# A streaming encoder on one core: super-blocks that begin with a row job, a planner with a slack, and a new order of jobs

## The chip, the cores and the metric

The kernel runs on one core of one Trainium2 chip. The metric is the device time of one execution in microseconds (us). Three runs of the kernel before gave 1244.92, 1247.65 and 1249.84 us; the median is 1247.65 us. Engines are named as in the profile: PE is TensorE's matmuls, PEld its weight loads, DVE VectorE, ACT ScalarE, POOL GpSimd, SP SyncE, which issues the DMAs.

## What is computed

One layer of an encoder with two parallel groups of heads: chunked attention (group A) and a gated recurrence (group B), for 2048 frames of a new stream (the prompt) and 64 frames of a running one (the sample).

```python
def mixer_layer(x, ln_g, w_in, lb, norm_g, w_out, attn_fn, s0):
    aq, ak, av, ag, hq, hf, hi, hg = jnp.split(rms_norm(x, ln_g) @ w_in, SPLITS, axis=-1)
    o_a = attn_fn(heads(aq), heads(ak), heads(av)).reshape(B, T, W_A) * jax.nn.silu(ag)
    o_b, S = hgrn2_branch(hq, hf, hi, hg, lb, norm_g, s0)
    return x + jnp.concatenate([o_a, o_b], axis=-1) @ w_out, k, v, S
```

`x` is 2112 rows of 1024 features, `w_in` is 1024 x 4096, `w_out` 1024 x 1024. Attention has 8 heads of 64; each chunk of 64 frames sees itself and 8 chunks before it, with a bias by distance; for the sample, 512 rows of keys and values come from a cache. The recurrence has 4 heads of 128 and works in blocks of 32 frames. A final RMS norm gives the outputs; new keys, values and states are outputs too. All is float32, to a precision that one pass of the float32r matmul does not reach: every operand is split into a high and a low part, and three products (high x high, low x high, high x low) are added.

## The kernel before

**Super-blocks.** The frames are worked in four super-blocks of 512 (`SUPER`, here 0 to 3); number 1 holds the 64 sample frames as well (576 columns, worked as 256 + 320, while the others are worked as 512). The normalised rows of a super-block are transposed into `xh` and `xl` (high and low part, 8 tiles of 128 features) by `x_tile` and `x_split`; a super-block is filled half by half.

**Jobs.** A job is one projection of 128 output features: 24 matmuls (3 products by 8 tiles of features) with the weight tile stationary, `project`. `hf`, `hq`, `hi`, `hg` are the recurrence's forget gate, query, input and output gate for head 0 to 3; `pq`, `pk`, `pv`, `pg` are queries, keys, values and gate of attention's head pair 0 to 3. A weight tile `w` holds high and low part, 1 MB; there are four (`WBUFS`). In super-block 0 the weights are read raw, split on VectorE and GpSimd, and kept in DRAM (`wd`, `wvd`); later super-blocks load them back. In super-blocks 1 to 3 the `pv` and `hi` jobs of two pairs and two heads are done together as a *row job* `rv0` or `rv1`, `project_rows`: there `x` is stationary and four weight tiles stream through, 512 columns at a time, so that the result has frames in its partitions. It needs all four weight tiles at once, goes over the frames in four tiles of 128 (two per half; in super-block 1 a sample pass lies between the halves) in *quarters* of 6 matmuls, and gives each weight tile back near its end. Its output goes through `row_out`: ScalarE copies it to a `sig` buffer and splits it to a `vT` buffer (two of each), and SyncE writes both to scratch in DRAM (`irow`, `vrow`), from where the recurrence (`gi`) and attention (`v`) load them. A buffer is free again when its DMA has landed.

**Which job uses which buffer.** Results wait in two PSUM banks `acc`. Jobs of kind h and `pg` are read out by ScalarE into `sig`; `pq` and `pk` into `vT`. The sample's key cache is loaded into `ck` and transposed on TensorE (`sample_cache`), for each head pair in super-block 1.

**What sets the order.** `JOBS` gives the order of the jobs by hand. The rest (recurrence, attention, transposes, output products) are Python generators that a planner, `Plan`, runs beside the jobs while the program is built: `main` walks through the jobs and `pump` lets every generator go on whose wanted time has come. The planner keeps a clock (`now`, TensorE's) and charges each instruction with an estimated cost; what it decides is fixed in the program as the order of the instructions of each engine. On the chip only semaphores count. `Tok` counts free buffers, with the planned time at which each is given back.

**The start of a super-block.** The first two jobs (`u < 2`) are worked by halves, first both jobs on half 0, then both on half 1, so that they can begin before the second half of `x` is there: `first`, line 2393. The last job of super-blocks 0 to 2 is worked by halves too.

Of the kernel before, what the change touches and what calls it, by code (L numbers as in the profile page):

```python
# [44 lines left out]

ROWSB = (1, 2, 3)
JOBS = [[(x[:2], int(x[2])) for x in jobs.split()] for jobs in (
# [8 lines left out]
)]  # L56


class Plan:
# [4 lines left out]

    LAG = {"": 0.0, "T": 200.0, "A": 100.0, "D": 100.0, "P": 100.0, "S": 100.0}
    TURN = 160.0

    def __init__(self):
        self.now = 0.0
        self.free = {"A": 0.0, "D": 0.0, "P": 0.0, "S": 0.0}  # L70
        self.done = {"A": 0.0, "D": 0.0, "P": 0.0, "S": 0.0}
        self.turns = {"D": [], "P": []}
        self.links = 0.0
        self.landed = 0.0
        self.mode = None
        self.run = 0
        self.breath = None
        self.threads = []
        self.count = 0
        self.rooms = {}  # L80
        self.seen = {}

    def spawn(self, gen, prio=1):
        self.count += 1
# [12 lines left out]
    def _when(self, want):  # L97


        if isinstance(want, tuple):  # L100
            return max(want[1], self.free[want[0]] - QUEUE)
        if isinstance(want, Tok):
            return want.when()
        return want

    def pump(self):
        moved = True
        any_ = False
        while moved:
            moved = False  # L110
            for th in list(self.threads):
                while self._ready(th[3]):
                    moved = any_ = True
                    try:
                        th[3] = next(th[2])
                        if th[3] is None:
                            th[3] = self.now + 1.0
                    except StopIteration:
                        self.threads.remove(th)
                        break  # L120
                if moved:
                    break
        return any_
# [6 lines left out]

    def main(self, gen):
        for want in gen:
            self.pump()
# [8 lines left out]
    def drain(self):  # L142
        while self.threads:
            if not self.pump():
                self.skip()
# [112 lines left out]
class Queue:  # L258
# [32 lines left out]
    def cost(self, name, aps, kw):  # L291
# [61 lines left out]
class Tok:  # L353


    def __init__(self, plan, n):
        self.plan = plan
        self.at = [0.0] * n

    @property  # L360
    def n(self):
        return sum(t <= self.plan.now for t in self.at)

    def when(self):
        return min(self.at) if self.at else NEVER

    def take(self):
        self.at.remove(min(self.at))
# [11 lines left out]
def hymba_step(  # L380
# [68 lines left out]
    def mm32(out, w, x):  # L449
        pe.matmul(out, w, x, start=True, stop=True)  # L450

    tk = {k: Tok(C, n) for k, n in dict(acc=2, s_ps=1, tr=2, pv=1, g=1, pr=PRB, ph=2, sig=2, vT=2, mixa=2,
                                     w=WBUFS, raw=RAWB, xn=XNB, qk=1, kv=1, q=1, sga=2, bias=1, gf=1, gi=1, gg=1,
                                     ck=1, slot=4, x4=0, x5=0, rec=1).items()}

# [351 lines left out]

    row_n = {}

    def project_rows(j, sb, r):  # L810


        ws = []
# [46 lines left out]
        for c0 in (0, 2 * P):  # L860
# [3 lines left out]
            steps = [(0, 0), (0, 1), (0, 2), (0, 3), (1, 0), (1, 1), (1, 2), (1, 3)]  # L864
            if c0:
                steps = [(0, 0), (0, 1), (0, 2), (1, 0), (1, 1), (0, 3), (1, 2), (1, 3)]
            for a, i in steps:
                c = c0 + a * P
                if a == len(accs):
                    yield from tk["acc"].get()  # L870
                    accs.append(acc_ps())
                yield from quarter(accs[a], c, i)
                if c0 and a:
                    tk["w"].put(1, C.pe())
                if i == 3:
                    C.spawn(row_out(sb, r, accs[a], c // P, C.pe()), 0)
# [1413 lines left out]
    def program():  # L2290
# [74 lines left out]
        for sb in range(nsb):  # L2365
# [6 lines left out]
            for u, (kind, g) in enumerate(JOBS[sb]):  # L2372
# [9 lines left out]
                            for c in range(off, off + bn, P):  # L2382
                                C.spawn(x_tile(sb + 1, half, c), 0.5)
                if kind == "rv":
                    yield from project_rows(j, sb, g)
                    j += 4
                    continue
                if (kind[0], g) not in made:
# [174 lines left out]
```

## Time and profile before

| | |
|---|---|
| runs | 1244.92, 1247.65, 1249.84 us |
| profiled execution | 1248.5 us, of which the span is 1246.7 us |
| mean granted clock of TensorE | 0.995 |
| DMA | 288.74 MB, 232 GB/s over the span |
| chain that ended last, by engine | PE 80%, DMA 5%, DVE 4%, the rest 1% each or less |

Nearly all instructions show one line (L273), since one helper records them; they are told apart by the tiles they write and read (out<-in). A row `MATMUL acc<-xh,w 128*128 128x512 f32` is a matmul into a bank of `acc` with 512 columns. Where matmuls follow each other the length of one (389 ns) is longer than the distance of their starts, since they are pipelined; what a matmul costs is read from the distance. Super-block 1 runs from about 260 us to about 545 us of the span.

### The profile page before, as it was taken

The numbers are of one execution on the slowest core, as the hardware profiler recorded it, in microseconds if no ns is written. First come the engines' busy times: TensorE is split into PE (matmuls) and PEld (weight loads), VectorE is DVE, ScalarE is ACT, GpSimd is POOL, SyncE is SP. The second block draws the span as 40 slices with busy tenths as digits, with TensorE's granted clock in tenths as the row PEclk, the third lists the DMA queues.
The fourth block names the chain that finished last, engine by engine and source line by source line (L and its number), as shares of the span: only waits on it lengthen the run. The fifth ranks groups of instructions, "written<-read, shape, count | busy, mean of one in ns | idle before, by whom it ended". The sixth has DMA issues, their size and how long they took to land.

```text
span 1246.7 us, 21739 instructions
## 1 busy us (share of the span) xinstructions
PE 1224.7 (98%) x7804; PEld 1062.6 (85%) x7804; DVE 894.6 (72%) x1864; ACT 694.6 (56%) x1520; POOL 374.3 (30%) x697
## 2 busy tenths in 40 slices
PE   9999999998999999999999999999999999999997
PEld 8788888988998899998888888998888888888786
DVE  7678887762876199798277857981878367887886
ACT  6344655552765187675357567772655446643443
POOL 7666647110122011111254541151112011741110
PEclk9999999998999999999999999999999999999999
DMA  8888996739354655542986797758454784997431
GB/s 294 276 277 310 313 323 215 256 105 329 126 190 161 227 177 200 193 137 93 382 306 220 273 368 279 259 200 310 186 175 165 250 322 162 362 308 203 127 135 68
DMA packets 126349, 288.74 MB, mean 232 GB/s; under 512 B 11745, under 2 KB 73057, under 8 KB 109602
## 3 DMA queue, kind: packets, MB, share of 16 engines
q1 hardware_dynamic: 126098, 287.09, 66.0%
q8 instruction: 62, 1.02, 0.3%
q14 instruction: 45, 0.37, 0.1%
q10 hardware_dynamic: 144, 0.26, 0.1%
HBM read 198.06 MB, written 90.83 MB: 232 GB/s over the span
## 4 chain that ended last, share of the span: by engine, by line
PE 80%; DMA 5%; DVE 4%; ACT 1%; POOL 1%; issue 1%; SPq 0%; DVEq 0%; ACTq 0%; POOLq 0%
PE acc L273 58%; PE g L273 7%; PE tr L273 6%; PE pv L273 5%; PE s L273 5%; POOL w L273 1%; DMA wraw<-in_w_in_dram 1%; DMA w<-wvd 1%; DMA ck<-in_cache_attn_k_dram 1%; DMA v<-vrow 1%; DVE xn L273 1%; DMA vrow<-vT 1%; DVE pr L273 1%; DMA w<-wd 1%; ACT sig L273 0%
## 5 line engine op out<-in xcount | busy, mean ns | idle before, releaser
L273 PE MATMUL acc<-xh,w 128*128 128x512 f32 (+2 forms) x2176 | 460.1, 351 | 3.1 <-ACT vT L273 2.3
L273 PEld LDWEIGHTS acc<-xh,w 128*128 128x128 f32 x2176 | 354.3, 190 | 46.4 <-ACT vT L273 2.5
L273 PE MATMUL acc<-xl,w 128*128 128x512 f32 (+2 forms) x1088 | 235.5, 350 | 0.0
L273 PEld LDWEIGHTS acc<-xl,w 128*128 128x128 f32 x1088 | 179.0, 191 | 21.7
L273 PE MATMUL acc<-w,xh 128*128 128x512 f32 x400 | 130.8, 396 | 1.7 <-DMA w<-wvd 1.7
L273 ACT ACTIVATE pr<-pr,nm 128x640 f32<-128x640 f32 (+4 forms) x132 | 100.4, 761 | 46.0 <-DVE nm L273 45.5
L273 ACT CAST ph<-tr 128x512 fp32r<-128x512 f32 (+3 forms) x176 | 87.2, 507 | 65.5 <-PE tr L273 33.0
L273 POOL TENSOR_TENSOR w<-wraw,w 128x256 fp32r<-128x256 f32 x120 | 104.4, 897 | 54.1 <-DVE w L273 31.9
L273 DVE CUSTOM_DVE_ANT_0 pr<-s,bias 128x640 f32<-128x640 f32 (+5 forms) x144 | 100.7, 703 | 21.2 <-PE s L273 20.4
L273 DVE TENSOR_TENSOR ph<-tr,ph 128x512 fp32r<-128x512 f32 (+3 forms) x176 | 101.3, 589 | 15.8 <-ACT ph L273 14.8
L273 PE MATMUL pv<-ph,v 128*128 128x256 f32 (+2 forms) x344 | 97.4, 373 | 0.5 <-DMA v<-vrow 0.2
L273 POOL TENSOR_TENSOR k<-ob 128x512 f32<-128x512 f32 (+2 forms) x20 | 18.2, 908 | 263.8 <-ACT ob L273 249.4
L273 ACT ACTIVATE sig<-acc 128x256 f32<-128x256 f32 (+2 forms) x87 | 42.9, 493 | 89.1 <-PE acc L273 86.0
L273 PE MATMUL tr<-ident,pr 128*128 128x128 f32 x580 | 89.0, 273 | 1.1 <-DVE ph L273 1.1
L273 PEld LDWEIGHTS acc<-w,xh 128*128 128x128 f32 x400 | 74.1, 188 | 16.4 <-DMA w<-wvd 2.6
L273 DVE TENSOR_SCALAR pr<-pr,sm 128x640 f32<-128x640 f32 (+4 forms) x132 | 79.6, 603 | 4.7
L273 PEld LDWEIGHTS tr<-ident,pr 128*128 128x128 f32 x580 | 70.0, 140 | 11.3 <-DVE ph L273 1.4
L273 PE MATMUL acc<-w,xl 128*128 128x512 f32 x200 | 78.3, 391 | 0.0
L273 POOL TENSOR_TENSOR mixa<-mixa,sga 128x256 f32<-128x256 f32 (+1 forms) x36 | 28.7, 796 | 131.2 <-DVE mixa L273 102.2
L273 DVE TENSOR_TENSOR mixa<-mixa,pv 64x256 f32<-64x256 f32 (+1 forms) x144 | 56.8, 395 | 14.1 <-ACT mixa L273 8.9
L273 PEld LDWEIGHTS pv<-ph,v 128*128 128x128 f32 x344 | 58.0, 189 | 9.7 <-issue 1.4
L273 ACT ACTIVATE sig<-sig 128x512 f32<-128x512 f32 (+2 forms) x110 | 57.7, 525 | 15.0 <-DVE gk L273 12.2
(326 smaller groups left out, 2209.0 us busy)
## 6 DMA issues: line engine op xcount, KB each, us to landing
w<-wd SPq DMA_DIRECT2D x72, 1024.0 KB, 6.6
wd<-w SPq DMA_DIRECT2D x24, 1024.0 KB, 6.9
w<-wvd SPq DMA_DIRECT2D x24, 1024.0 KB, 5.0
wraw<-in_w_in_dram SPq DMA_DIRECT2D x30, 512.0 KB, 5.4
wod<-xn SPq DMA_DIRECT2D x28, 512.0 KB, 5.6
v<-vrow SPq DMA_DIRECT2D x24, 512.0 KB, 7.8
xn<-in_x_prompt_dram SPq DMA_DIRECT2D x23, 512.0 KB, 5.5
wvd<-w SPq DMA_DIRECT2D x16, 512.0 KB, 7.0
```

Of the source, the lines that this page charges most:

```text
L273: r = f(*args, **kw)
```

## The change

Four edits. The order of the jobs is new, and super-blocks 1 to 3 begin with `rv0`. The first two jobs of a super-block that begins so are not worked by halves any more; the row job itself goes, in its first half, over both tiles of frames for each weight tile in turn. The planner holds a thread's wanted time and the return of PSUM banks back by 200 ns (`MARGIN`), unless nothing else can be issued. And GpSimd's instructions with two inputs are charged more in the planner's table of costs above 257 columns.

```diff
-    "hf0 hq0 rv0 hg0 pq0 pk0 hf1 pg0 hq1 hg1 pg1 hf2 pq1 hq2 rv1 pk1 hg2 pg2 pq2 pk2 hq3 hg3 pg3 hf3 "
-    "pk3 pq3",
+    "rv0 hf0 hg0 pg0 pq0 hq0 pk0 hf1 hq1 hg1 pg1 pk1 pq1 rv1 hf2 hq2 pg2 pq2 pk2 hg2 hf3 hq3 pq3 hg3 "
+    "pg3 pk3",
...
+    MARGIN = 200.0
+    BANKS = ("acc", "s_ps", "tr", "pv", "g")
...
-        return want
+        return want + self.margin
...
-                            th[3] = self.now + 1.0
+                            th[3] = ("", self.now + 1.0)
...
         for want in gen:
+            self.margin = self.MARGIN
             self.pump()
             while not self._ready(want):
                 if not self.pump() and not self._ready(want):
+                    if self.margin:
+                        self.margin = 0.0
+                        continue
...
-            return min(200.0 + 2.1 * n, 432.0 + 1.2 * n), 43.0 if n > 128 else 66.0, True
+            pairs = name in ("tensor_tensor", "tensor_mul", "tensor_sub")
+            return (200.0 + 2.1 * n if pairs else min(200.0 + 2.1 * n, 432.0 + 1.2 * n)), 43.0 if n > 128 else 66.0, True
...
-        return sum(t <= self.plan.now for t in self.at)
+        return sum(t + self.late() <= self.plan.now for t in self.at)
...
             if c0:
                 steps = [(0, 0), (0, 1), (0, 2), (1, 0), (1, 1), (0, 3), (1, 2), (1, 3)]
+            elif first:
+                steps = [(a, i) for i in range(4) for a in range(2)]
...
-                first, end = u < 2, not last and u >= len(JOBS[sb]) - 1
+                first, end = u < 2 and JOBS[sb][0][0] != "rv", not last and u >= len(JOBS[sb]) - 1
```

Where this moves instructions is seen in three places. The names are tiles with the building's numbers; L273 of the kernel before and L281 of the changed one are the same helper.

**First place: the loads and the cache's transposes behind `rv0` of super-block 1.** SyncE's DMAs, before, from the first load of head pair 0 on (`kd` keys, `v` values, `bias`, `ck` the key cache, `w` a weight tile, `gi` the recurrence's input):

```order
L273 DMA kd_3475<-carry_0_18_91 128x2x512
L273 DMA v_3478<-vrow_30_103 128x1024
L273 DMA bias_3481<-biasd_40_113 128x1280
L273 DMA ck_3485<-in_cache_attn_k_dram 128x4x128
L273 DMA w_3494<-wd_56_129 128x2048
L273 DMA gi_3431<-irow_35_108 128x512
L273 DMA gi_3431<-ilast_112 64x128
L273 DMA v_3478<-vrow_31_104 128x1024
```

and in the changed kernel:

```order
L281 DMA w_3299<-wd_60_133 128x2048
L281 DMA gi_3249<-irow_35_108 128x512
L281 DMA gi_3249<-ilast_112 64x128
L281 DMA kd_3365<-carry_0_18_91 128x2x512
L281 DMA v_3368<-vrow_30_103 128x1024
L281 DMA v_3368<-vrow_31_104 128x1024
L281 DMA v_3368<-vlast_111 64x256
L281 DMA bias_3373<-biasd_40_113 128x1280
L281 DMA ck_3377<-in_cache_attn_k_dram 128x4x128
```

A weight tile, the recurrence's input and the second part of `v` now stand ahead of `ck`. TensorE's rows up to the transposes of `ck`, before (the job `acc_3545` is the second half of the second job behind the row job):

```order
L273 MATMUL acc_3545<-xh_168,w_3382 128x320 x2
L273 MATMUL g_3552<-ident_71,bl_3249 128x128 x2
L273 MATMUL acc_3545<-xh_168,w_3382 128x320 x6
L273 MATMUL acc_3545<-xl_169,w_3382 128x320 x8
L273 MATMUL acc_3545<-xh_168,w_3382 128x320 x4
L273 MATMUL tr_3577<-ident_71,ck_3485 128x128 x4
```

and in the changed kernel, where `acc_3379` and `acc_3411` are the two blocks of the third job behind the row job and `acc_3442` begins the fourth (the two jobs ahead of them stand without anything between):

```order
L281 MATMUL acc_3379<-xh_168,w_3218 128x256 x8
L281 MATMUL acc_3379<-xl_169,w_3218 128x256 x8
L281 MATMUL acc_3379<-xh_168,w_3218 128x256 x8
L281 MATMUL acc_3411<-xh_168,w_3218 128x320 x8
L281 MATMUL acc_3411<-xl_169,w_3218 128x320 x8
L281 MATMUL acc_3411<-xh_168,w_3218 128x320 x8
L281 MATMUL acc_3442<-xh_168,w_3228 128x256 x8
L281 MATMUL acc_3442<-xl_169,w_3228 128x256 x8
L281 MATMUL acc_3442<-xh_168,w_3228 128x256 x8
L281 MATMUL acc_3474<-xh_168,w_3228 128x320 x4
L281 MATMUL tr_3481<-ident_71,ck_3377 128x128 x4
```

The transposes moved from the second job behind the row job to the fourth.

**Second place: ScalarE behind `rv1` of super-block 1.** Before, after the last two outputs of the row job (`sig` and `vT` from `acc`), the key job `pk1` follows:

```order
L273 COPY sig_5052<-acc_4999 128x512
L273 CAST vT_5054<-sig_5052 128x2x2x64
L273 COPY sig_5071<-acc_5027 128x512
L273 CAST vT_5073<-sig_5071 128x2x2x64
L273 COPY vT_5133<-acc_5076 128x256
L273 CAST kd_4414<-vT_5133 64x256 x2
```

and in the changed kernel the forget gate `hf2`:

```order
L281 COPY sig_5225<-acc_5101 128x512
L281 CAST vT_5227<-sig_5225 128x2x2x64
L281 COPY sig_5249<-acc_5156 128x512
L281 CAST vT_5251<-sig_5249 128x2x2x64
L281 ACTIVATE sig_5287<-acc_5246 128x256
L281 ACTIVATE sig_5287<-sig_5287,one_79 128x256
```

The first read-out behind the row job now takes a `sig` buffer where it took a `vT` buffer.

**Third place: TensorE at the start of super-block 2.** Before, `hf0` (`acc_6813`) and `hq0` (`acc_6878`) on half 0, 256 columns, with transposes (`tr`, `g`) and attention scores (`s`) between:

```order
L273 MATMUL acc_6813<-xh_168,w_6380 128x256 x6
L273 MATMUL tr_6824<-ident_71,xn_6701 128x128 x4
L273 MATMUL acc_6813<-xh_168,w_6380 128x256 x2
L273 MATMUL acc_6813<-xl_169,w_6380 128x256 x6
L273 MATMUL s_6848<-kd_6281,q_6282 128x320 x2
L273 MATMUL s_6848<-kd_6281,ql_170 128x320 x2
L273 MATMUL acc_6813<-xl_169,w_6380 128x256 x2
L273 MATMUL acc_6813<-xh_168,w_6380 128x256 x8
L273 MATMUL g_6872<-ident_71,xn_6701 128x128 x4
L273 MATMUL acc_6878<-xh_168,w_6499 128x256 x8
```

and in the changed kernel the first quarters of `rv0`, 512 columns, on two tiles of frames (`acc_6844`, `acc_6889`):

```order
L281 MATMUL acc_6844<-w_6382,xh_168 128x512
L281 MATMUL acc_6844<-w_6382,xl_169 128x512
L281 MATMUL g_6872<-ident_71,bl_6725 128x128 x2
L281 MATMUL g_6872<-ident_71,bl_6725 64x128
L281 MATMUL acc_6844<-w_6382,xh_168 128x512
L281 MATMUL acc_6844<-w_6382,xl_169 128x512
L281 MATMUL acc_6844<-w_6382,xh_168 128x512 x2
L281 MATMUL acc_6889<-w_6382,xh_168 128x512
L281 MATMUL acc_6889<-w_6382,xl_169 128x512
```

The eight pieces of `hf0` and `hq0` by halves are gone from the start; these jobs follow behind the row job with 512 columns. In the whole program TensorE has 192 matmuls of 256 columns less and 96 of 512 columns more; no other form changes its count.

More of the change, by code (lines that the diff above doesn't have):

```diff
@@ L66 @@
     TURN = 160.0
+    MARGIN = 200.0
+    BANKS = ("acc", "s_ps", "tr", "pv", "g")
     def __init__(self):
         self.now = 0.0
-        self.free = {"A": 0.0, "D": 0.0, "P": 0.0, "S": 0.0}
+        self.free = {"": 0.0, "A": 0.0, "D": 0.0, "P": 0.0, "S": 0.0}
         self.done = {"A": 0.0, "D": 0.0, "P": 0.0, "S": 0.0}
@@ L132, in main @@
         for want in gen:
+            self.margin = self.MARGIN
             self.pump()
@@ L142, in drain @@
     def drain(self):
+        self.margin = 0.0
         while self.threads:
@@ L353, with __init__, late @@
 class Tok:
-    def __init__(self, plan, n):
+    def __init__(self, plan, n, bank=False):
         self.plan = plan
+        self.bank = bank
         self.at = [0.0] * n
+    def late(self):
+        return self.plan.margin if self.bank else 0.0
     @property
     def n(self):
-        return sum(t <= self.plan.now for t in self.at)
+        return sum(t + self.late() <= self.plan.now for t in self.at)
     def when(self):
-        return min(self.at) if self.at else NEVER
+        return min(self.at) + self.late() if self.at else NEVER
     def take(self):
@@ L450, in mm32 @@
         pe.matmul(out, w, x, start=True, stop=True)
-    tk = {k: Tok(C, n) for k, n in dict(acc=2, s_ps=1, tr=2, pv=1, g=1, pr=PRB, ph=2, sig=2, vT=2, mixa=2,
+    tk = {k: Tok(C, n, k in C.BANKS) for k, n in dict(acc=2, s_ps=1, tr=2, pv=1, g=1, pr=PRB, ph=2, sig=2, vT=2, mixa=2,
                                      w=WBUFS, raw=RAWB, xn=XNB, qk=1, kv=1, q=1, sga=2, bias=1, gf=1, gi=1, gg=1,
@@ L808, in hymba_step, with project_rows @@
     row_n = {}
-    def project_rows(j, sb, r):
+    def project_rows(j, sb, r, first):
         ws = []
@@ L2384, in program @@
                 if kind == "rv":
-                    yield from project_rows(j, sb, g)
+                    yield from project_rows(j, sb, g, u == 0)
                     j += 4
```

12 rows, old and new, of the table JOBS are left out of this document.

## The prediction

> **What bounds the kernel now.** I read the page first.
>
> ```profile
> span 1246.7 us, 21739 instructions
> PE 1224.7 (98%) x7804; PEld 1062.6 (85%) x7804; DVE 894.6 (72%) x1864; ACT 694.6 (56%) x1520; POOL 374.3 (30%) x697
> ```
>
> TensorE (PE) is busy for 98% of the span; the next engine, VectorE, for 72%. So the time is TensorE's work plus the 22 us in which it stands still, and a part of that is the start and the end of the program. A change of order can win only standing time and cheaper forms of the same matmuls. Next I read who TensorE waits for (columns: waiting tile, releaser, us in total, times, longest).
>
> ```profile
> PE tr L273 <- DMA ck<-in_cache_attn_k_dram: 3.3, 1, 3.3
> PE acc L273 <- ACT vT L273: 2.3, 1, 2.3
> PE acc L273 <- DMA w<-wvd: 1.7, 2, 1.1
> PE s L273 <- DVE nm L273: 1.4, 4, 0.8
> PE tr L273 <- DVE ph L273: 1.1, 2, 0.8
> PE g L273 <- POOL breath L458: 1.1, 1, 1.1
> PE g L273 <- DVE asb L273: 1.0, 2, 0.6
> PE acc L273 <- DVE xn L273: 0.9, 2, 0.5
> PE acc L273 <- ACT sig L273: 0.8, 1, 0.8
> PE g L273 <- ACT k L273: 0.4, 1, 0.4
> ```
>
> These ten rows add up to 14.0 us, and three waits (3.3, 2.3, 1.1) are nearly half of it. All three lie in super-block 1. The timeline of TensorE gives their places (start, length, instructions, then the idle time ahead in brackets), the windows the clock that was granted around them (window, its length, PE busy, PEclk, DMA share, GB/s).
>
> ```profile
> 287.88 1.19 PE L273 MATMUL acc<-xh,w 128*128 128x256 f32 x8
> ...
> 301.23 0.75 PE L273 MATMUL acc<-xh,w 128*128 128x320 f32 x4
> 305.31 1.11 PE L273 MATMUL tr<-ident,ck 128*128 128x128 f32 x4 [3.33 <-DMA ck<-in_cache_attn_k_dram]
> ...
> 400.52 0.50 PE L273 MATMUL acc<-w,xh 128*128 128x512 f32 x1 [1.12 <-DMA w<-wvd]
> ...
> 421.97 1.12 PE L273 MATMUL acc<-xh,w 128*128 128x256 f32 x8
> ...
> 426.02 1.34 PE L273 MATMUL acc<-xl,w 128*128 128x320 f32 x8
> 427.19 1.33 PE L273 MATMUL acc<-xh,w 128*128 128x320 f32 x8
> 430.80 1.59 PE L273 MATMUL acc<-xh,w 128*128 128x256 f32 x6 [2.27 <-ACT vT L273]
> ```
>
> ```profile
> 302.00:306.00 4.00, 0.69 (x3) 0.83 1.03 405
> 306.00:310.00 4.00, 4.00 (x20) 0.50 0.81 249
> 310.00:314.00 4.00, 4.00 (x29) 0.82 0.50 202
> 398.00:402.00 4.00, 2.88 (x13) 1.00 0.56 229
> 429.00:433.00 4.00, 2.20 (x10) 0.74 1.04 412
> 433.00:437.00 4.00, 4.00 (x56) 0.84 0.52 174
> ```
>
> Each of the two long waits is followed by a stretch at half clock. Its length is (1 - PEclk) / 0.5 x 4 us, summed: 1.36 + 4.00 + 1.44 = 6.80 us after the first, 2.08 + 1.28 = 3.36 us after the second. The first began at 306 - 1.36 = 304.64 and TensorE stood idle until 305.31, so 6.13 us of work ran at half speed and lost 3.07 us; the second lost 1.68 us. The wait of 1.12 us has no such tail (398.00:402.00).
>
> The rows at 287.88 and 421.97 are the first job behind a row job each: the row jobs end there.
>
> What ended the three waits is in the chain of waits (start, us, what).
>
> ```profile
> 294.81 10.46 DMA ck<-in_cache_attn_k_dram
> 395.32 5.16 DMA w<-wvd
> 421.22 9.06 DMA vrow<-vT
> ```
>
> The cause is the same at 294.81 and 421.22: both lie just behind a row job. Its four weight tiles come free almost together, four loads of 1 MB fill the queue (DMA share 1.03), and the transfer that is needed next stands behind them.
>
> **The change part by part. Halves.** In super-blocks 2 and 3 the first two jobs now run in halves of 256 columns; behind a row job they run as one of 512. Four jobs of 48 matmuls become four of 24: 192 matmuls of 256 columns out, 96 of 512 in (super-block 1 is cut in two anyway).
>
> ```profile
> 422.93 1.12 PE L273 MATMUL acc<-xl,w 128*128 128x256 f32 x8
> 423.89 2.30 PE L273 MATMUL acc<-xh,w 128*128 128x256 f32 x16
> 1095.34 54.55 PE acc L273 x240
> ```
>
> Starts at 422.93 and 423.89 with 8 matmuls between give 120 ns for 256 columns; 54.55 / 240 gives 227.3 ns for 512 (the last row is of the chain). 192 x 120 - 96 x 227.3 = 23.04 - 21.82, so **-1.22 us**. TensorE is the bound there, so nothing hides it.
>
> The Trainium skill, "TensorE: Matmul & The Clock Gate", section "Wait — 56ns, not 53.3ns?", gives a warm matmul N / 2.4 GHz plus about 2.5 ns, which makes two halves only 2.5 ns dearer than one whole; by that rule this term would be 0.24 us and the sum 1.0 us higher. The trace has 120 and 227 ns, and I go by the trace.
>
> **The wait at 430.80.** The row job's outputs sit in the two `sig` and two `vT` buffers until their DMAs to scratch land. In the present order a key job (`pk1`) follows the second row job of super-block 1 and needs `vT` at once.
>
> ```profile
> 291.92 0.39 ACT L273 ACTIVATE sig<-acc 128x256 f32<-128x256 f32 x1 [2.96 <-DMA irow<-sig]
> ...
> 430.38 0.37 ACT L273 COPY vT<-acc 128x256 f32<-128x256 f32 x1 [7.18 <-DMA vrow<-vT]
> ```
>
> ScalarE waited 7.18 us for `vrow<-vT`, both banks of `acc` stayed full, TensorE stopped. In the new order every row job is followed by jobs of kind h; the ScalarE rows shown above (second place) have `sig` there. `sig` waits for `irow<-sig`, which cost ScalarE 2.96 us at 291.92 and TensorE nothing. So this wait goes, with its clock: 2.27 + 1.68 = **-3.95 us**. Late next is `irow`: the third rival.
>
> The same page of the Trainium skill, section "What's actually happening", lets the clock fall only after an idle window of about 3.4 us. By that rule 2.27 us would not have done it, and this term would be 2.27 alone, the sum 1.7 us higher. The rows at 429 and 433 show that it did, so I price waits over 2 us with their clock.
>
> **The wait at 305.31.** `ck` stays behind the weight loads, and the SyncE rows shown above put one weight load and one `v` load more ahead of it. But its transposes move back. Before, TensorE came to them at 301.98, 14.1 us after the row job's end (287.88). Now three whole jobs and more lie between: a job of super-block 1 is 24 x 120 ns + 24 x 146 ns (8 matmuls of 320 columns from 426.02 to 427.19) = 6.39 us, so 3 x 6.39 + 2.88 + 4 x 0.146 = 22.6 us. `ck` landed at 305.27, 17.4 us after the row job; 1.5 MB more at the 405 GB/s of the window make 21.1 us. It is there 1.5 us early, as an estimate. So 3.33 + 3.07 = **-6.40 us** goes. The second row job of super-block 1 now has the same train behind it, `ck` again on its end, at about the same distance. An estimate that is 1.5 us early can miss: bounds are 0 and 6.40 us for each of the two, and I take 0.5 each, **+1.0 us**, nearer to the row worked out.
>
> **The wait at 400.52.** The fourth weight tile of that row job took 5.16 us from its slot's release and was waited for 1.12, so only some 4 us of work lay between. In the new order more work lies between: **-1.12 us**. Row jobs at a start run their two halves' quarters in turn and need the fourth tile after six quarters in place of three.
>
> **The slack.** 200 ns between the planned end of an operand and its use on TensorE can remove short waits for VectorE and ScalarE: `nm`, `ph`, `asb`, `k` are 3.9 us in 9 waits. At most 9 x 0.2 = 1.8; below, a gain can be lost where the plan then finds other work out of turn. I take the middle, **-0.9 us**.
>
> **New waits.** Any new order has some of its own. The trace cannot show them; bounds are 0 and one long wait with its clock (6.40). I take one of the common size, **+1.12 us**.
>
> The corrected cost of GpSimd's two-operand instructions in the planner and job order 0 move work that is not on TensorE's path (POOL is busy 30%): nothing, within the last bound. Sum, against the profiled execution's 1248.5 us (span 1246.7 plus 1.8): 1248.5 - 1.22 - 3.95 - 6.40 - 1.12 - 0.9 + 1.0 + 1.12 = **1237.0 us**. The median of the three runs is 0.85 us lower than that execution; I leave the sum as it is, inside their spread of 4.9.
>
> **The rivals.** *The queue wins again.* `ck` or another load is still late behind four weight loads, at one or both row jobs of super-block 1. For it: DMA shares of 1.03 and 1.04, and two loads more ahead of it. Against: 22.6 us of work in place of 14.1. One such wait with its clock gives 1237.0 + 6.4 - 0.5 = 1242.9, two 1248.8.
>
> *The change does not do what it says.* The slack and the order only rename the waits, since transfers are late by microseconds and the slack is 0.2. Left is the halves' term: 1247.3.
>
> *Slower: `irow` blocks ScalarE.* ScalarE works in order, and the first activation of the second job after a row job waits until the last `irow<-sig` has landed.
>
> ```profile
> 298.38 0.32 SPq L273 DMA_DIRECT2D gi<-irow  x1
> 433.47 0.33 SPq L273 DMA_DIRECT2D gi<-irow  x1
> ...
> 293.33 0.42 DVE L273 TENSOR_TENSOR gg<-acc,sig 128x256 f32<-128x256 f32 x1 [3.91 <-ACT sig L273]
> ```
>
> The two loads start when `irow` is there: 10.5 us after the row job's end (287.88), and 11.5 after 421.97. TensorE needs that bank again two jobs after the row job, 2 x 6.39 = 12.8 us, and freeing it takes 1.83 us (291.92 to the end of VectorE's product, 293.75). So it decides from 11.0 us on, and super-block 1 stands right at that point. If all six row jobs lost what 430.80 lost, 6 x 3.95 = 23.7 on 1248.5 - 13.6 = 1234.9 makes 1258.6. Against it: jobs of super-blocks 2 and 3 are 24 x 227 ns x 2 = 10.9 us for two, so the bank has the more time, and `irow` would have to land as late as 14 us after the row job.
>
> **How the numbers follow.** Forecast 0.63, between 1231 (no new wait, all short ones gone: 1234.9 - 3.0, less the 0.85 of the median) and 1241; still faster 0.01; the queue again 0.20; no effect 0.10; `irow` 0.06. 0.5% of the median is 6.2 us, about what a measurement can tell, so faster ends at 1241.4 and slower starts at 1253.9. The forecast alone lies below 1241.4; queue and no effect lie within. The range reaches from 1231 to no effect, 1247.5, and leaves out `irow`, both queue waits and the 0.01: under 0.2.
>
> **What would show it.** Right: no wait over 2 us on TensorE, PEclk 1.00 from the start to the tail, no row `acc <- ACT vT`, PE busy lower by about 1.2 us and by what the clock cost (4.75). Wrong: a row `tr <- DMA ck` of over 2 us, PEclk below 1 in super-block 1, or `acc <- ACT sig` just behind the row jobs. What would upset it all is another burst of loads that I have not counted, in super-block 2 above all, where the output weights move too.

## The result, and the profile after

Six executions of the changed kernel gave a median of 1237.75 us (1236.63 to 1242.66), six of the kernel before 1248.01 us. The ratio is 0.9925, with a 95% interval of 0.9903 to 0.9946: faster by 0.75%. The forecast was 1237.0 us. How the forecast comes to be so near is a longer story than its sum tells.

The profiled execution took 1236.75 us, of which the span is 1235.0 us. The first lines of its page:

```profile
span 1235.0 us, 21510 instructions
PE 1217.7 (99%) x7708; PEld 1052.2 (85%) x7708; DVE 889.2 (72%) x1851; ACT 692.2 (56%) x1506; POOL 377.2 (31%) x705
```

TensorE is busy for 7.0 us less than before (1224.7) and stands still for 17.3 us in place of 22.0. Whom it waits for (waiting tile, releaser, us in total, times, longest):

```profile
PE g L281 <- DVE k L281: 1.8, 3, 0.8
PE s L281 <- DVE nm L281: 1.7, 2, 1.1
PE tr L281 <- DVE ph L281: 1.3, 2, 1.1
PE acc L281 <- DMA w<-wvd: 1.2, 1, 1.2
...
PE pv L281 <- DVE mixa L281: 1.0, 1, 1.0
```

The two long rows of before, `tr <- DMA ck` and `acc <- ACT vT`, are gone. The waits for VectorE, all rows of the view added, are 6.0 us; before they were 5.4. Super-block 1 is best read in windows of 50 us (window, its length, TensorE busy, granted clock, DMA share, GB/s). The kernel before:

```profile
300.00:350.00 50.00, 46.67 (x361) 0.93 0.49 173
400.00:450.00 50.00, 47.21 (x302) 0.97 0.51 183
```

and the changed one, with a third window that the experiments need:

```profile
300.00:350.00 50.00, 50.00 (x434) 1.00 0.41 139
400.00:450.00 50.00, 50.00 (x353) 1.00 0.66 238
530.00:555.00 25.00, 25.00 (x192) 1.00 0.25 84
```

In these two windows TensorE stood still for 3.33 + 2.79 = 6.1 us and lost at most 50 x (0.07 + 0.03) = 5.0 us to the clock (4.75 by the prediction's closer reading, since the clock costs nothing while TensorE stands). Both are zero now: some 11 of the 11.7 us by which the span is shorter. TensorE's busy time fell by 7.0 us where the prediction had 1.22 + 4.75 = 5.97.

Behind the first row job of super-block 1 the timeline of the changed kernel (start, length, instructions) shows the end of the row job and the cache's transposes, on TensorE, and on SyncE the load; the view of DMA issues (size, us to landing) shows when that landed.

```profile
275.15 0.61 PE L281 MATMUL acc<-w,xh 128*128 128x512 f32 x2
...
298.42 0.60 PE L281 MATMUL tr<-ident,ck 128*128 128x128 f32 x4
```

```profile
290.90 0.43 SPq L281 DMA_DIRECT2D ck<-in_cache_attn_k_dram  x1
```

```profile
ck<-in_cache_attn_k_dram SPq DMA_DIRECT2D x1, 256.0 KB, 7.3
```

The row job ends at about 275.7. The transposes stand 22.7 us behind it (forecast 22.6), `ck` landed at 290.9 + 7.3 = 298.2. It was 1.5 us early by my estimate; it was early by some 0.2 us.

### The profile page after: what moved, and what is told of

It reads as the page before. It is cut to its first block, busy times and chain, and to the rows that moved or that the text cites. A ratio compares the mean times of both kernels' runs of the same rounds, so it can differ in the third digit from the quotient of the medians.

```text
span 1235.0 us, 21510 instructions
## 1 busy us (share of the span) xinstructions
PE 1217.7 (99%) x7708; PEld 1052.2 (85%) x7708; DVE 889.2 (72%) x1851; ACT 692.2 (56%) x1506; POOL 377.2 (31%) x705
## 4 chain that ended last, share of the span: by engine, by line
PE 86%; DVE 6%; ACT 3%; DMA 3%; issue 1%; POOL 1%; SPq 0%; DVEq 0%; POOLq 0%; ACTq 0%
PE acc L281 63%; PE g L281 7%; PE tr L281 6%; PE pv L281 5%; PE s L281 5%; DVE pr L281 1%; POOL w L281 1%; DVE xn L281 1%; DVE q L281 1%; DVE k L281 1%; DMA w<-wvd 1%; DMA xn<-in_x_prompt_dram 1%; ACT sig L281 1%; DMA carry<-kd 1%; DVE ph L281 0%
## 5 line engine op out<-in xcount | busy, mean ns | idle before, releaser
L281 PE MATMUL acc<-xh,w 128*128 128x512 f32 (+2 forms) x2112 | 448.4, 353 | 1.0 <-ACT sig L281 0.8
L281 PEld LDWEIGHTS acc<-xh,w 128*128 128x128 f32 x2112 | 346.3, 189 | 46.2 <-ACT sig L281 1.0
L281 PE MATMUL acc<-xl,w 128*128 128x512 f32 (+2 forms) x1056 | 232.2, 353 | 0.0
L281 PEld LDWEIGHTS acc<-xl,w 128*128 128x128 f32 x1056 | 173.7, 189 | 21.7
L281 PE MATMUL acc<-w,xh 128*128 128x512 f32 x400 | 134.6, 402 | 1.2 <-DMA w<-wvd 1.2
L281 ACT ACTIVATE pr<-pr,nm 128x640 f32<-128x640 f32 (+4 forms) x132 | 100.4, 761 | 50.7 <-DVE nm L281 50.3
L281 ACT CAST ph<-tr 128x512 fp32r<-128x512 f32 (+3 forms) x176 | 87.6, 507 | 63.3 <-PE tr L281 33.7
L281 DVE TENSOR_TENSOR ph<-tr,ph 128x512 fp32r<-128x512 f32 (+3 forms) x176 | 101.6, 590 | 25.0 <-ACT ph L281 24.0
L281 POOL TENSOR_TENSOR w<-wraw,w 128x256 fp32r<-128x256 f32 x120 | 102.7, 885 | 47.1 <-DVE w L281 27.5
L281 DVE CUSTOM_DVE_ANT_0 pr<-s,bias 128x640 f32<-128x640 f32 (+5 forms) x144 | 100.7, 703 | 16.1 <-PE s L281 15.5
L281 ACT ACTIVATE sig<-acc 128x512 f32<-128x512 f32 (+1 forms) x82 | 42.1, 514 | 112.7 <-PE acc L281 105.3
L281 PE MATMUL pv<-ph,v 128*128 128x256 f32 (+2 forms) x344 | 95.1, 367 | 1.0 <-DVE mixa L281 1.0
L281 PE MATMUL tr<-ident,pr 128*128 128x128 f32 x580 | 88.0, 273 | 1.3 <-DVE ph L281 1.3
L281 POOL TENSOR_TENSOR mixa<-mixa,sga 128x256 f32<-128x256 f32 (+1 forms) x36 | 28.8, 800 | 197.6 <-DVE mixa L281 177.0
L281 PEld LDWEIGHTS acc<-w,xh 128*128 128x128 f32 x400 | 73.3, 188 | 14.4 <-DMA w<-wvd 1.5
L281 PEld LDWEIGHTS tr<-ident,pr 128*128 128x128 f32 x580 | 70.2, 140 | 14.7 <-DVE ph L281 2.9
L281 DVE TENSOR_SCALAR pr<-pr,sm 128x640 f32<-128x640 f32 (+4 forms) x132 | 78.9, 598 | 4.7
L281 PE MATMUL acc<-w,xl 128*128 128x512 f32 x200 | 78.5, 393 | 0.0
L281 PEld LDWEIGHTS pv<-ph,v 128*128 128x128 f32 x344 | 59.3, 189 | 10.3 <-ACT slot L281 1.4
L281 DVE TENSOR_TENSOR mixa<-mixa,pv 64x256 f32<-64x256 f32 (+1 forms) x144 | 56.9, 395 | 15.5 <-ACT mixa L281 12.0
L281 ACT ACTIVATE sig<-sig 128x512 f32<-128x512 f32 (+2 forms) x103 | 56.0, 546 | 15.8 <-DVE gk L281 13.2
L281 POOL TENSOR_TENSOR k<-ob 128x512 f32<-128x512 f32 (+2 forms) x20 | 18.7, 934 | 143.5 <-ACT ob L281 141.5
```

What stands on the lines that cost most here:

```text
L281: r = f(*args, **kw)
```

## The experiments

Each result is a median with its ratio to executions of the kernel before on the same chip (1247.2 to 1248.4 us). My theory is the sum of the prediction: the order mends super-block 1, the slack is small. The main rival is that the slack carries the gain.

### One wait at a time in the kernel before

```diff
-    ... hf2 pq1 hq2 rv1 pk1 hg2 pg2 ...
+    ... hf2 pq1 hq2 rv1 hg2 pk1 pg2 ...
```

> The kernel before with one pair of jobs exchanged in super-block 1: behind its second row job comes hg2, then pk1, in place of pk1, then hg2. Theory A (the wait of 2.27 us at 430.80 came from vT, held by vrow on its way to scratch, and the half clock behind it cost 1.68 us more): the row acc <- ACT vT over 2 us is gone, PEclk is 1.00 between 425 and 440 us, the wait of 3.33 us for ck and its half clock stay, and the time falls by 3.95 us, to about 1244.1 from 1248.0. Rival B (the queue only names another victim): a wait of 1 us or more for sig, w or ck stands within 20 us behind the same row job, and the time stays within 1 us of 1248.0. Rival C (the lower clock has nothing to do with the wait): the wait goes and some microseconds at half clock near 430 us stay, 1245.7.

Measured: 1255.41 us, ratio 1.0073 (1.0051 to 1.0096). No theory forecast that it would be slower. From the timeline of TensorE behind the second row job, and the windows there:

```profile
432.89 0.98 PE L273 MATMUL g<-gi,k 128*128 128x128 f32 x4 [1.93 <-ACT pr L273]
```

```profile
428.00:432.00 4.00, 2.51 (x42) 1.00 0.97 362
432.00:436.00 4.00, 3.10 (x13) 0.64 0.03 9
436.00:440.00 4.00, 4.00 (x30) 0.93 0.00 0
```

The wait for `vT` is gone, and one of 1.93 us for the recurrence stands 2 us further on, with half clock behind it. That is Rival B in kind, though the operand is not one that it named and the time did not stay within 1 us. The rest of the loss lies where the exchange has no business: `w<-wvd` is waited for 3.3 us in place of 1.7 (one wait of 2.17 us in super-block 2), and the waits for VectorE grow from 5.4 to 7.8 us. The planner lays out everything behind an exchange anew.

Ahead of the exchange TensorE's instructions are the same as in the kernel before. Yet the timeline there is another:

```profile
289.16 1.19 PE L273 MATMUL acc<-xh,w 128*128 128x256 f32 x8 [0.97 <-DMA w<-wd]
...
304.48 0.66 PE L273 MATMUL tr<-ident,ck 128*128 128x128 f32 x4 [1.23 <-DMA ck<-in_cache_attn_k_dram]
```

Here the weight tile behind the first row job is late, and `ck` by 1.23 us instead of 3.33, with no half clock (the window 300 to 350 is at 1.00). So the 6.40 us that the prediction reads from one execution are 2.2 us in another execution of the same instructions, and Theory A's "stays" did not hold either.

```diff
+                if sb == 1 and u == 1:
+                    C.spawn(ck_load(0), 0)
...
-        yield from tk["ck"].get()
-        ck = T(wk, [P, 4, P], F32, "ck", bufs=1)
-        sp.dma_start(ck, cache_k[:, p * P : (p + 1) * P].rearrange("(t q) d -> q t d", q=P))
-        t = C.dma(300)
+        if p not in ck_early:
+            yield from ck_load(p)
+        ck, t = ck_early[p]
```

(`ck_load` holds the lines taken out.)

> The kernel before with one edit: the first load of ck in super-block 1 is issued ahead of the row job and its four weight loads. Theory A (ck was late because it stood last in the queue behind those loads): no wait for ck, PEclk 1.00 between 300 and 315 us, the wait of 2.27 us at about 430 us stays, and the time falls by 3.33 + 3.07 = 6.40 us, to about 1241.6 from 1248.0. Rival B (the whole queue is late, not ck alone): bias, v or gi is waited for within the next 20 us, and the time falls by less than 2 us. Rival C (the clock falls there for another reason): the wait goes, the half clock stays, and the time falls by 3.3 us.

Measured: 1248.64 us, ratio 1.0002 (0.9985 to 1.0019): nothing. From the timeline of TensorE behind the two row jobs, and a window there:

```profile
289.18 1.19 PE L273 MATMUL acc<-xh,w 128*128 128x256 f32 x8 [1.71 <-DMA w<-wd]
...
426.68 1.21 PE L273 MATMUL acc<-xh,w 128*128 128x256 f32 x8 [2.66 <-ACT vT L273]
```

```profile
428.00:432.00 4.00, 4.00 (x59) 1.00 0.73 261
```

No wait for `ck` is left, but the weight tile behind the row job is waited for 1.71 us, and `w<-wvd` for 3.3 us (2.30 of them in super-block 2). By the time this is Rival B, but the early load did not do it: it was issued at 240.94 and took 5.5 us, so that it had landed 35 us before the four weight loads began, and the exchanged jobs of above had the same tile 0.97 us late without it. That tile's wait differs from execution to execution; that the full queue took another victim is not shown. Against the 2.2 us of that run a gain of 0.5 us is left at this place, less than twelve executions can tell. And the 2.66 us for `vT` have no half clock behind them: the window after is at 1.00.

### The order alone, and the planner alone

The next is the kernel before with the new `JOBS`, the flag `first` and the alternating quarters; the planner is that of before. Against the changed kernel:

```diff
-    MARGIN = 200.0
+    MARGIN = 0.0
...
-            return (200.0 + 2.1 * n if pairs else min(200.0 + 2.1 * n, 432.0 + 1.2 * n)), 43.0 if n > 128 else 66.0, True
+            return min(200.0 + 2.1 * n, 432.0 + 1.2 * n), 43.0 if n > 128 else 66.0, True
...
-                            th[3] = ("", self.now + 1.0)
+                            th[3] = self.now + 1.0
```

> The kernel before with the new job orders and the row job first, and nothing of the planner changed (no slack, old cost of GpSimd): the edits to the order alone. The new order without slack, but with the new cost, took 1252.5 us, with 16.4 us of waits for VectorE and hardly any lost at 300 to 350 and 400 to 450 us, the two places in super-block 1 that the order was to mend. Theory A (without slack this order is planned too tight, whatever the costs): 1249 to 1256, over 12 us of waits for VectorE, none over 2 us at the two places. Theory B (the 1252.5 us were chance of one plan): 1236 to 1244, waits for VectorE about 5 us as in the kernel before.

Measured: 1255.15 us, ratio 1.0052 (1.0034 to 1.0071). **The order by itself makes the kernel slower**, as Theory A has it. Its windows:

```profile
300.00:350.00 50.00, 50.00 (x434) 1.00 0.39 138
400.00:450.00 50.00, 50.00 (x349) 1.00 0.63 218
530.00:555.00 25.00, 19.99 (x122) 0.86 0.30 104
```

Super-block 1 is mended just as in the changed kernel. But the start of super-block 2 loses 5.0 us standing and some 2 us of clock (at most 25 x 0.14 = 3.5, and a good part of that half clock falls into the standing), and waits for VectorE are 15.3 us in all. The chain of waits at that place (start, us, what):

```profile
537.16 0.89 PE tr L281 x8
...
538.07 3.68 DMA xn<-in_x_prompt_dram
...
541.86 1.16 ACT ck L281 x2
...
543.61 1.29 DVE xn L281
```

and the timeline of TensorE:

```profile
544.95 1.97 PE L281 MATMUL tr<-ident,xn 128*128 128x128 f32 x8 [2.65 <-DVE xn L281]
...
549.75 0.48 PE L281 MATMUL acc<-w,xh 128*128 128x512 f32 x1
```

The last rows of `x` for super-block 2 are loaded when transposes give their buffer back, at 538.07; the load, ScalarE's sum of squares and VectorE's normalising then run one after the other while TensorE has no job. The changed kernel issues this load 10.7 us earlier and begins the row job at 535.13 (14.6 us earlier), from its timelines of SyncE and TensorE:

```profile
527.38 0.33 SPq L281 DMA_DIRECT2D xn<-in_x_prompt_dram  x1
```

```profile
535.13 0.39 PE L281 MATMUL acc<-w,xh 128*128 128x512 f32 x1
```

The two spans differ by 18.1 us, and by the pages 9.8 of them are standing time and 8.3 longer busy time (1226.0 and 1217.7). Half clock accounts for some 2 of the 8.3. A matmul's length (389 ns) is longer than its distance to the next one (227 ns), so a break of up to some 160 ns counts as busy; that the rest is such breaks fits, but no view lists them.

The same without slack, but with the new cost of GpSimd:

```diff
-    MARGIN = 200.0
+    MARGIN = 0.0
```

> The changed kernel with MARGIN = 0 in place of 200: the new order of jobs without the slack. Theory A (the gain is that of the order, the slack takes 0.9 us of short waits, at most 1.8): 1238.6, no more than 1240; no wait over 2 us in super-block 1. Rival B (the slack carries the gain, the order alone would not have it): 1244 or more, with waits for VectorE and ScalarE by 5 us or more above those of the changed kernel. Rival C (the slack does nothing, and what it does to the order is chance): 1236 to 1240, with no more short waits than the changed kernel has.

Measured: 1252.45 us, ratio 1.0047 (1.0029 to 1.0065). Rival B: 16.4 us of waits for VectorE, and both windows of super-block 1 at 50.00 and 1.00.

The opposite: the changed kernel with the job orders of before, so that halves come back.

> The changed kernel with the job orders of the kernel before, so that the first two jobs are in halves again: only the slack and the corrected cost of GpSimd's instructions with two inputs are left. Theory A (order first): the waits of over 2 us behind the row jobs of super-block 1 are still there, and the time is 1248.0 - 0.9 = 1247.1, between 1246 and 1249. Rival B (the slack carries the gain): 1243 or less, and the short waits for nm, ph, asb and k are half of what they were (7.3 us beside the three long ones).

Measured: 1243.05 us, ratio 0.9966 (0.9953 to 0.9979); 4 to 5 us are gained, which is nearer to Rival B, but not by its mechanism: waits for VectorE are 7.5 us, more than the 5.4 of before. Nor is its standing time much shorter (21.5 and 22.0 us by the pages): the gain lies in TensorE's busy time, 1219.3 for 1224.7 us, of which half clock (3.44 us in place of 10.2) accounts for a part. Its two waits in super-block 1, and the windows behind them:

```profile
304.55 0.66 PE L281 MATMUL tr<-ident,ck 128*128 128x128 f32 x4 [1.88 <-DMA ck<-in_cache_attn_k_dram]
...
428.54 1.21 PE L281 MATMUL acc<-xh,w 128*128 128x256 f32 x8 [2.35 <-ACT vT L281]
```

```profile
304.00:308.00 4.00, 3.45 (x18) 0.65 1.03 388
308.00:312.00 4.00, 4.00 (x31) 0.92 0.95 339
428.00:432.00 4.00, 3.46 (x28) 1.00 0.96 375
```

Both long waits stand, as Theory A has it. The shorter one has half clock behind it, the longer one has none.

### How much slack

```diff
-    MARGIN = 200.0
+    MARGIN = 100.0
```

> The changed kernel with MARGIN = 100. The new order without slack took 1252.5 us with 16.4 us of TensorE's waits for VectorE, with 200 ns 1237.8 us with 6.0 us. Theory A (the slack by its size removes waits for VectorE): between the two, about 1245, with some 11 us of waits for VectorE. Theory B (each plan falls by chance, and this order was picked with the plan of 200 ns): a time anywhere between 1238 and 1253 that follows no order of the slacks; 1252 or more, or 1240 or less, speaks for B.

Measured: 1239.04 us, ratio 0.9925 (0.9902 to 0.9947), with 4.6 us of waits for VectorE. Theory A's 1245 and 11 us are out; by the expectation, 1240 or less speaks for Theory B, chance of the plan.

```diff
-    MARGIN = 200.0
+    MARGIN = 400.0
```

> The changed kernel with MARGIN = 400. Theory A (the slack by its size removes waits for VectorE): 6.0 us of such waits become 4 or less, 1235 to 1238. Theory B (chance of the plan): new waits of 1 us and more at places that the changed kernel has none at, 1240 to 1250. Theory C (too much slack holds work back): TensorE finds less to issue, jobs run out ahead of the recurrence and attention, and the time lost stands at the ends of the super-blocks, over 1245.

Measured: 1251.88 us, ratio 1.0039 (1.0020 to 1.0058). Theory A is out. There are new waits of over 1 us, as Theory B has it, and the time is over that theory's range, as Theory C has it; the runs do not part the two. Its longest wait is at the start of super-block 1, and again for rows of `x`:

```profile
240.57 0.66 PE L281 MATMUL tr<-ident,xn 128*128 128x128 f32 x4 [3.18 <-DVE xn L281]
```

The old job orders (that of `e4_old_jobs`) with `MARGIN = 400`:

> The job orders of the kernel before with MARGIN = 400 and the corrected cost of GpSimd. With 200 ns these orders took 1243.1 us, with waits for VectorE of 7.5 us (kernel before, no slack: 5.4), so that there the slack did not take such waits away. Theory A (slack by its size): below 1243, waits for VectorE below 7. Theory B (chance of the plan): 1243 to 1250, and the waits behind the row jobs of super-block 1 stay as they were or move, by no rule.

Measured: 1250.57 us, ratio 1.0022 (1.0005 to 1.0039): Theory A is out, and the time is just over Theory B's range. All plans side by side (waits of TensorE for VectorE in the profiled execution, their sum and how many the view lists; 0* and 200* have the old cost of GpSimd, 200* is the run of the next section):

| orders | slack, ns | median, us | waits for VectorE, us | how many |
|---|---|---|---|---|
| new | 0* | 1255.15 | 15.3 | 23 |
| new | 0 | 1252.45 | 16.4 | 24 |
| new | 100 | 1239.04 | 4.6 | 9 |
| new | 200 | 1237.75 | 6.0 | 9 |
| new | 200* | 1236.77 | 3.6 | 8 |
| new | 400 | 1251.88 | 15.1 | 16 |
| old | 0* | 1248.01 | 5.4 | 14 |
| old | 200 | 1243.05 | 7.5 | 14 |
| old | 400 | 1250.57 | 12.5 | 18 |

With the new orders two plans without slack are bad, three with 100 and 200 ns are good, and 400 ns is bad with either order. So it is not one single lucky plan. But the new order was picked with the planner at 200 ns, as an expectation above says, and one exchanged pair of jobs alone moved the time by 8 us: that 100 to 200 ns are good for any order, and do not only fit this one, is not shown. Nor does the slack merely take its own length off each wait: from 0 to 200 ns 15 of 24 waits for VectorE go, with 10.4 us, 0.7 us each in the mean, 10 of them under 1 us. With 400 ns the number stays lower, but longer waits come.

### The cost of GpSimd's instructions

```diff
-            return (200.0 + 2.1 * n if pairs else min(200.0 + 2.1 * n, 432.0 + 1.2 * n)), 43.0 if n > 128 else 66.0, True
+            return min(200.0 + 2.1 * n, 432.0 + 1.2 * n), 43.0 if n > 128 else 66.0, True
```

> The changed kernel with the planner's old cost of GpSimd's instructions with two inputs; order and slack stay. Theory A (that cost is worth nothing by itself, as I took it, and a plan with the same slack is as good): 1236 to 1240. Theory B (chance of the plan: any change of a planned time reshuffles the rest): 1240 to 1250, with waits of 1 us or more at new places. Theory C (the cost matters where VectorE waits for GpSimd): the time is higher, and new waits of TensorE for VectorE stand behind idle time of VectorE that GpSimd ended.

Measured: 1236.77 us, ratio 0.9901 (0.9879 to 0.9923), Theory A. The cost is worth nothing, and a neighbouring plan with the same slack is as good.

### Halves, twelve times over

```diff
-                first, end = u < 2 and JOBS[sb][0][0] != "rv", not last and u >= len(JOBS[sb]) - 1
-                two = (first and 2 == 2) or (end and 1 == 2)
+                first, end = u < 2 and not sb or sb > 1, not last and u >= len(JOBS[sb]) - 1
+                two = not sb and u < 2
```

> The changed kernel with every job of super-blocks 2 and 3 but the row jobs worked by halves: 1128 matmuls of 512 columns become 2256 of 256, twelve times what the change itself does. Theory A (pitches of the trace, 120 and 227.3 ns): 2256 x 0.120 - 1128 x 0.2273 = 14.3 us more, 1252 from 1237.8, with PE busy higher by about as much and no wait over 2 us. Rival B (the rule of the Trainium skill, TensorE: Matmul & The Clock Gate, a matmul is N / 2.4 GHz and some 2.5 ns): 2.8 us more, 1240.6. Rival C (half jobs give the banks back earlier and so take waits away): under 1240.

Measured: 1274.41 us, ratio 1.0209 (1.0186 to 1.0231), 36.7 us more where 14.3 were forecast. The pitch is right, from the timeline of TensorE:

```profile
711.63 2.08 PE L281 MATMUL acc<-xh,w 128*128 128x256 f32 x16
713.55 1.12 PE L281 MATMUL acc<-xl,w 128*128 128x256 f32 x8
```

Sixteen matmuls take 713.55 - 711.63 = 1.92 us, 120 ns each. What I missed are waits, which Theory A excluded:

```profile
PE acc L281 <- DVE gq L281: 6.4, 2, 5.0
PE acc L281 <- DVE sga L281: 3.3, 3, 1.7
PE acc L281 <- DVE gg L281: 1.9, 2, 1.1
```

All three are read-outs of banks by VectorE: a half job fills a bank in half the time. By the spans of the two profiled executions (1273.5 and 1235.0) there are 38.5 us more; all waits grow from 10.7 to 27.7, and 10.2 us at half clock (windows of 4 us, added) cost at most 5.1. That leaves 38.5 - 17.0 - 5.1 = 16.4 us or a little more for the matmuls, near to 14.3 and far from Rival B's 2.8.

### The place of `ck` in the queue

```diff
+        for i, x in enumerate(burden if p == 0 else ()):
+            sp.dma_start(x, wd[i][:, 0])
         sp.dma_start(ck, cache_k[:, p * P : (p + 1) * P].rearrange("(t q) d -> q t d", q=P))
```

(`burden`: three DRAM tiles of 0.5 MB.)

> The changed kernel with three copies of 0.5 MB from DRAM to DRAM issued just ahead of the first ck of super-block 1; the order on every engine but SyncE is the same. In the changed kernel ck landed at 298.16 and its transposes began at 298.42. Theory A (ck's place in the queue sets it, and it has 0.3 us to spare): 1.5 MB at 405 GB/s make ck 3.7 us later, if the writes count beside the reads 7.4; the wait is 3.4 to 7.1 us, and the half clock behind such a wait costs 0 to 3.4 us more: 1241 to 1248, about 1243. Rival B (the queue has room, or the work behind covers it): 1237.8, no wait for ck over 0.7 us.

Measured: 1243.79 us, ratio 0.9965 (0.9945 to 0.9985), about what Theory A said, but not by its wait. From the issues and the timeline:

```profile
ck<-in_cache_attn_k_dram SPq DMA_DIRECT2D x1, 256.0 KB, 9.8
```

```profile
292.61 0.45 SPq L281 DMA_DIRECT2D ck<-in_cache_attn_k_dram  x1
```

```profile
302.47 0.66 PE L281 MATMUL tr<-ident,ck 128*128 128x128 f32 x4
```

`ck` landed at 302.4, 4.2 us later (1.7 since SyncE issued it later, 2.5 since it took longer), so its place in the queue does set it. But the expectation was wrong that TensorE's order would stay: the planner charges every DMA, and set the transposes 4.05 us later. No wait for `ck` came of it. What was lost is waits for VectorE and ScalarE, some 3 us between 300 and 400 us, and 1.1 us more for `w<-wvd`. How dear a late `ck` is in this order, the run does not tell.

The changed kernel with the old cost of GpSimd and the early `ck` of the second experiment:

> The changed kernel with the old cost of GpSimd (1236.8 us) and the first ck of super-block 1 loaded ahead of the row job; TensorE's order is nearly that of the run with the old cost. Theory A (ck was just in time in these plans, 0 to 1.2 us early, so that an early load takes away a wait in some executions only): median 1236 to 1237.5, the highest execution under 1239. Rival B (the early load takes room from the loads of the row job, as in the kernel before, where the wait moved to the weights): 1239 or more, with w<-wvd or w<-wd waits of 1 us or more in super-block 1.

Measured: 1237.03 us (1235.46 to 1238.61), ratio 0.9908 (0.9887 to 0.9928). The transposes stand at 286.74 now, and nothing moved to the weights of super-block 1. It does as Theory A says. But against the run that it edits (1236.77) nothing is gained, the 0.7 us on the changed kernel lie within the intervals of both, and six executions do not show that the high one (1242.66) came of `ck`. No run beats the changed kernel by more than can be told.

## Why the prediction was right, and where it was not

**Super-block 1 is right.** The changed kernel and all six runs with the new orders, up to 200 ns of slack and no burden on the queue show 50.00 of 50.00 at clock 1.00 in both windows; every run with the old orders keeps the wait for `vT` or one in its place. That was the core of the sum, 3.95 + 6.40 + 1.12 = 11.47 us, as one execution of the kernel before had it; the run with exchanged jobs shows 2.2 us where that execution lost 6.40, so the size of this term is that execution's. The signs that the prediction named came too: the longest wait of the changed kernel's TensorE is 1.2 us, and its windows show no half clock before 1232 us.

**But not as single waits to be taken off.** Taken one at a time, the two waits gave a loss of 8 us and nothing at all. With the jobs exchanged, another wait came in place of the one taken off; with the early `ck`, the wait for the weight tile ate most of what was to be gained, and that wait differs between executions. That the new order wins by spreading the whole train, the row job's outputs, the loads and their users, is how I read it, and not shown by itself.

**`ck`.** The distance, 22.6 us, was 22.7. That `ck` would be 1.5 us early was too much (0.2). Nor is it the order of jobs alone that sets the distance: the planner puts the transposes where it expects the load to land, as the burdened run shows. In the old order it was wrong by 3.33 us in one execution and by 1.23 in another, here by next to nothing; two other plans of the new order, without slack and with 100 ns, wait for `ck` by 0.3 to 0.6 us.

**The wait at 400.52.** The weight tile that was late in super-block 1's second row job is not waited for any more, but the same wait stands at the second row job of super-block 2 (1.2 us). Over the program `w<-wvd` went from 1.7 to 1.2: -0.5, not -1.12.

**The step that failed: the slack and the new waits.** The forecast was -0.9 ("at most 9 x 0.2 = 1.8") and +1.12 ("bounds are 0 and one long wait with its clock (6.40)"). Measured apart, the new order without slack stands at 1255.15: with the forecast's 1237.0 + 0.9 = 1237.9, 17 us are left that only the term of the new waits can hold, and the slack then takes off 1255.15 - 1236.77 = 18.4 us, not 0.9 (between two chips whose kernels before differ by 1.2 us). Both terms left their bounds, with opposite signs, and their sum, +0.2, came out right: that is luck. The reason for the slack's bound was false: a slack does not shorten a listed wait by its length, and nine waits of one trace are not all that it acts on. It changes what the planner issues next, and so when the rows of `x`, on a chain of DMA, ScalarE and VectorE, are ready at the start of a super-block. The chain at 538 us shows this for one place; why 200 ns are enough there, and 400 harm elsewhere, the runs leave open. So the change is neither its order nor its slack: the order alone loses 7 us, the planner alone gains 5, both gain 10.

**Halves.** 1.22 us is borne out by the pitch and, twelvefold, by what is left of 38.5 us (16.4 for 14.3).

**The clock.** 4.75 us is what that one profiled execution lost, and the profile after does not lose it. For the medians it is too much: the exchanged run went through the first of the two places at full clock, and the mean granted clock was 0.9972 over 59 executions of the kernel before beside the experiments, and 0.9977 over the 6 of the changed one, 0.0005 x 1240 = 0.6 us. The profiled execution of before had an unusually low clock (0.995) and a usual time, so it must have lost less elsewhere than most. Where the others lose more, no profile shows. So 1237.0 came this near to the median of 1237.75 in part by luck here too.

**The rivals.** *The queue wins again* did not come, by 0.2 us; *irow* did not either. ScalarE's waits behind the first row job of super-block 1 (270 to 310 us) have it:

```profile
ACT sig L281 <- DMA irow<-sig: 4.1, 2, 2.4
```

TensorE waits for nothing there. *The change does not do what it says* is refuted for super-block 1.

## What to carry to other kernels

Where a planner lays out the program, an edit cannot be priced wait by wait from the old trace: the sum holds for the place that the edit was made for, and the rest of the program is dealt anew. So measure order and planner apart and together, and try the planner's number on both sides: here 0 and 400 ns lose what 100 to 200 ns gain. And a wait that one profile shows behind a burst of loads can be about a third as long in another execution of the same instructions: before pricing it, look at a second profile.

## What the runs showed of the hardware

The length of a wait does not decide whether the clock falls. Waits of 1.88 us (old orders with slack, at 304) and 1.93 us (exchanged jobs, at 432) were followed by half clock, waits of 2.35 and 2.66 us were not. At one place, the second row job of super-block 2, a wait of 2.62 us in the run with the old cost of GpSimd (at 672) had no half clock behind it, and one of 2.41 us in the run with the early `ck` (at 671) had 3.44 us of it. Where it fell, the stretch was the same: (1 - 0.65) / 0.5 x 4 + (1 - 0.92) / 0.5 x 4 = 3.44 us in the rows at 304 to 312, 3.44 us in those at 432 to 440, 3.36 and about twice that, 6.80, in the kernel before. One such stretch costs half of its length in which TensorE works, at most 1.7 us. The Trainium skill, "TensorE: Matmul & The Clock Gate", section "What's actually happening", says that the clock is judged over windows of 3413 ns that run freely and are not set by the kernel. The stretches agree with that length, and the missing link to the wait's length with the free running; that a whole window must be idle, these waits do not bear out. I had priced each wait over 2 us with its clock; 0 to 3.4 us, by chance, would have been right.
